# Splitting the first matmul groups by rows of x as they land, and a tail with two adding DMAs

## The chip, the cores and the metric

One program runs on all 8 cores of one Trainium2 chip, each core with one sequence of its own. The metric is the device time of the slowest core in microseconds (us). All times here are of fast runs: executions in which one die is slower than the other at a lower clock, as the program sometimes has them, are left out. A core's *span* is the time from its first to its last instruction in the records; the time of an execution was 1.5 to 2.7 us above its longest span.

## The reference, cut to what matters

One layer of a decoder trunk. Each core takes 2080 tokens of 1024 channels:

```python
h = rmsnorm(x, g_pre_mix)
z = h @ w_in                          # 4096 columns: u, v, b, c and two gates
...                                   # pooling mixer and gated short convolution, merged by gates
x = x + rmsnorm(merged @ w_o, g_post_mix)
h = rmsnorm(x, g_pre_ffn)
upc, new_ffn = causal_dwconv(h @ w_up, buf_ffn, w_ffn_conv)     # 2 x 2816 columns
gate, val = jnp.split(upc, 2, axis=-1)
y = (jax.nn.silu(gate) * val) @ w_down
x = x + rmsnorm(y, g_post_ffn)
```

## The kernel before

Channels lie on the partitions. A tile of x is 8 rows (k = 0 to 7) of 128 channels. In the mixer the tokens come in five tiles (512, then 392 each). A group is 8 matmuls, one for each k, into one PSUM bank. The first five groups of tiles 0 and 1 use x scaled but not yet normed (`RAW`), so they don't wait for the sums of squares.

```python
def win_group(t, jj, b, lo, hb):
    N = TA[t]
    wb = W_IN.ap[:, jj, :].rearrange("p (k c) -> p k c", k=KC)
    pe([(bank(b, N, lo), wb[:, k, :], hb.ap[:, k, lo:N]) for k in range(KC)], [W_IN.t(jj, 1), hb.t()],
       [("ps", b)], N - lo)
...
wd = [wload(W_IN, w_in, 0, 1, BL)]
wd += [wload(W_IN, w_in, i, 1, BL, after=[xs0[1]]) for i in range(1, 16)]   # after x's second pair of rows
...
seq = [(0, i) for i in range(NRAW, M0)] + [(1, i) for i in range(NRAW)] + [(0, i) for i in range(M0, M1)]
for t, i in seq:
    F_block(t, i)          # one group each, and its eviction
```

PE's order is fixed, so the first group of tile 1 stands still until all 8 rows of tile 1's x have landed and are converted, and all that follows waits behind it. The first group behind the 40 matmuls of tile 1 is tile 0's ninth; its start is the end of the head.

The weights of the second half (`w_up`, 44 blocks of 256 KB) are loaded block by block while the last mixer tiles run:

```python
def wup(n):
    ...
    pool_dma(dst.flat, w_up[:, i * BL:k * BL], [], [dst.t()], 128 * (k - i) * BL * 4, mx=2048,
             after=[last_pe[0]])
```

The tail of the last tile multiplies 8 rows of y by the norm and adds the residual: two rows by an adding DMA (GpSimd issues it, the DMA adds to what lies in memory), six by adds on DVE and POOL with plain writes behind them:

```python
for q in range(4):
    yq = Y.ap[:, 2 * q:2 * q + 2, :]
    dve(... out=yq, in0=yq, in1=sdb, op=ALU.mult ...)
    if q == 0:
        pool_dma(yT[:, 0:2, lo:lo + NB], yq, ..., acc=True)
        continue
    for k, n, add in ((2 * q, 2, (pool_tt, dve)[q - 1]),) if q < 3 else ((6, 1, dve), (7, 1, pool_tt)):
        add(... out=yk, in0=yk, in1=X1.ap[:, k:k + n, :], op=ALU.add ...)
        sp_dma(yT[:, k:k + n, lo:lo + NB], yk, ...)
```

Of the kernel before, what the change touches and what calls it, by code (L numbers as in the profile page):

```python
# [62 lines left out]
class Sched:  # L63
# [55 lines left out]
    def order(self):  # L119
# [29 lines left out]
        tab = None  # L149
# [130 lines left out]
def build_nc():  # L280
# [257 lines left out]
    def prenorm_sq(t, q):  # L538
        sq = XSQ2[0] if t == 0 else H[t]
        N = TA[t]  # L540
        act(lambda e: e.activation(out=sq.ap[:, 2 * q:2 * q + 2, 0:N], in_=X[t].ap[:, 2 * q:2 * q + 2, :], func=AF.Square),
            [X[t].t(2 * q, 2)], [sq.t(2 * q, 2)], 2 * N)

# [16 lines left out]
    def win_group(t, jj, b, lo, hb):  # L560
        N = TA[t]
        wb = W_IN.ap[:, jj, :].rearrange("p (k c) -> p k c", k=KC)
        pe([(bank(b, N, lo), wb[:, k, :], hb.ap[:, k, lo:N]) for k in range(KC)], [W_IN.t(jj, 1), hb.t()],
           [("ps", b)], N - lo)
# [83 lines left out]
    def F_block(t, i):  # L648
        kind, c = FSEQ[i]
        N = TA[t]  # L650
        lo = lo_of(t, {"u": 0, "b": LO}.get(kind, LOP))
        raw = t < 2 and i < NRAW
        b = next_bank()
        win_group(t, i, b, lo, RAW[t] if raw else H[t])
# [200 lines left out]
    def epi_y(t):  # L855
# [7 lines left out]
        if t == NTB - 1:  # L863
            for q in range(4):
                yq = Y.ap[:, 2 * q:2 * q + 2, :]
                dve(lambda e, yq=yq: e.tensor_tensor(out=yq, in0=yq, in1=sdb, op=ALU.mult),  # L866
                    [Y.t(2 * q, 2), ("ps", SB)], [Y.t(2 * q, 2)], 2 * NB, psum=True, pri=-40000.0 + 4000 * q)
                if q == 0:
                    pool_dma(yT[:, 0:2, lo:lo + NB], yq, [Y.t(0, 2)], [("yo", t, q)], 2 * 128 * 2 * NB * 4, acc=True)
                    continue  # L870
                for k, n, add in ((2 * q, 2, (pool_tt, dve)[q - 1]),) if q < 3 else ((6, 1, dve), (7, 1, pool_tt)):
                    yk = Y.ap[:, k:k + n, :]
                    add(lambda e, yk=yk, k=k, n=n: e.tensor_tensor(out=yk, in0=yk, in1=X1.ap[:, k:k + n, :], op=ALU.add),  # L873
                        [Y.t(k, n), X1.t(k, n)], [Y.t(k, n)], n * NB)
                    sp_dma(yT[:, k:k + n, lo:lo + NB], yk, [Y.t(k, n)], [("yo", t, k)], 128 * n * NB * 4)
# [24 lines left out]
    def warm(n):  # L900
# [4 lines left out]
    xs0 = [sp_dma(X[0].flat[:, 0:2 * N0], xT[0][:, 0:2 * N0], [], [X[0].t(0, 2)], 128 * 2 * N0 * 4,  # L905
                  pri=-1e6)]
    sp_dma(CST, cst, [], [KCST], 128 * 256 * 4, pri=-9e5)
    for q in range(1, 4):
        xs0.append(sp_dma(X[0].flat[:, 2 * q * N0:2 * (q + 1) * N0], xT[0][:, 2 * q * N0:2 * (q + 1) * N0], [],
                          [X[0].t(2 * q, 2)], 128 * 2 * N0 * 4, pri=-8e5 + q))  # L910
# [4 lines left out]
    wd += [wload(W_IN, w_in, i, 1, BL, after=[xs0[1]]) for i in range(1, 16)]  # L915
# [10 lines left out]
    for q in range(4):  # L926
        prenorm_sq(0, q)
        for k in (2 * q, 2 * q + 1):
            dve(lambda e, k=k: e.tensor_scalar(out=RAW[0].ap[:, k, :], in0=X[0].ap[:, k, :], scalar1=cc(C_G1 + k), scalar2=None,
                                               op0=ALU.mult), [X[0].t(k, 1), KCST], [RAW[0].t(k, 1)], N0, rate=2.0)  # L930
    for q in range(4):
        pe([(bank(SB, N0), ONES, XSQ2[0].ap[:, k, :]) for k in (2 * q, 2 * q + 1)], [ONESB.t(), XSQ2[0].t(2 * q, 2)],
           [("ps", SB)], N0, start=q == 0, stop=q == 3)
        if q < 3:
            warm(20)
    ln_exp(0, N0, sq=1)
    for i in range(NRAW):
        F_block(0, i)
# [14 lines left out]
    for i in range(NRAW, 16):  # L953
        seq += [(1, i)] + ([(0, M1 + i - NRAW)] if M1 + i - NRAW < 16 else [])
    for t, i in seq:
        F_block(t, i)
# [225 lines left out]
```

## Time and profile before

| | before |
|---|---|
| time, median of the first runs | 826.05 us (825.92 to 827.45) |
| the profiled execution | 824.09 us, spans 816.9 to 822.5 us |
| start of tile 0's ninth group, by core | 39.1 to 44.9 us, mean 41.6 |
| PE's idle time before tile 1 | 1.5 to 4.4 us, mean 3.0 |
| from that start to the end of the last matmul | 766.6 to 768.7 us, mean 767.1 |
| tail: from there to the last landing | 10.6 to 11.0 us |

The last three rows of times sum to a core's span but for some 0.3 us. They are read from the trace core by core: **head**, **middle**, **tail**. The page itself shows the slowest core alone.

### The profile page before, as it was taken

The page shows a single profiled execution, that of the slowest core. Times are in us where ns is not written, and L with a number is a line of the kernel's source. Part 1 is how long each engine was busy: PE and PEld are TensorE (multiplying, and loading weights), DVE is VectorE, ACT ScalarE, POOL GpSimd, SP SyncE. Part 2 cuts the span into 40 slices and gives each one's busy share as a digit, 9 for nine tenths or more (in the row PEclk, how much of TensorE's full clock was granted, in tenths as well). Part 3 has the DMA queues.
Part 4 walks back from the last instruction along what each step waited for, and adds up shares of the span by engine and source line. Part 5 has one row for each costly group of instructions (what it writes and reads, how often), then busy time and mean ns, then how long its engine had stood idle before and what let it go on. Part 6 is the DMA issues. An engine that isn't in the chain of part 4 may idle for free.

```text
span 822.5 us, 16751 instructions; the slowest of 8 cores (816.9 to 822.5 us)
## 1 busy us (share of the span) xinstructions
PE 799.4 (97%) x5138; PEld 499.5 (61%) x5138; DVE 565.1 (69%) x1054; ACT 452.1 (55%) x902; POOL 262.8 (32%) x297
## 2 busy tenths in 40 slices
PE   6799999999999999999999999999999999999994
PEld 5355445555555555666666666666666666666662
DVE  3788438896895867688996476568566765785723
ACT  3333265666565555676765475456556554665532
POOL 5543001001201243489642243225222522242231
PEclk9899999999999999999999999999999999999998
DMA  8999803845125789999970033015101500050063
GB/s 164 200 159 155 145 25 89 214 130 129 64 75 102 140 135 216 202 161 158 195 128 1 16 56 61 1 36 70 37 2 36 70 2 1 3 68 2 1 136 74
DMA packets 62839, 75.18 MB, mean 91 GB/s; under 512 B 3072, under 2 KB 59264, under 8 KB 62736
## 3 DMA queue, kind: packets, MB, share of 16 engines
q0 software_dynamic: 41440, 44.97, 37.9%
q1 hardware_dynamic: 21312, 29.14, 11.7%
q8 instruction: 44, 0.72, 0.3%
q14 instruction: 43, 0.35, 0.2%
HBM read 81.53 MB, written 22.90 MB: 127 GB/s over the span
## 4 chain that ended last, share of the span: by engine, by line
PE 94%; DMA 3%; POOL 1%; DVE 1%; issue 0%; DVEq 0%; ACT 0%; SPq 0%; ACTq 0%; POOLq 0%
PE ps L469 94%; DMA big<-xT 3%; POOL big L482 1%; DVEq L1053 0%; DVE big L866 0%; DVE big L784 0%; ACT big L849 0%; SPq L476 0%; DVE big L822 0%; ACT big L524 0%; ACT ps L527 0%; DVE big L947 0%; DVE big L873 0%; DVEq L272 0%; ACTq L272 0%
## 5 line engine op out<-in xcount | busy, mean ns | idle before, releaser
L469 PE MATMUL ps<-big 128*128 128x346 bf16 (+6 forms) x5138 | 799.4, 319 | 12.1 <-DVE big L947 4.4
L469 PEld LDWEIGHTS ps<-big 128*128 128x128 bf16 x5138 | 499.5, 98 | 311.8 <-issue 18.4
L822 DVE SCALAR_TENSOR_TENSOR big<-ps,big 128x344 f32<-128x344 f32 (+1 forms) x528 | 281.4, 569 | 95.3 <-ACT big L818 74.6
L836 POOL TENSOR_TENSOR big<-big 128x344 bf16<-128x344 f32 x132 | 125.3, 950 | 257.1 <-DVE big L822 181.2
L818 ACT ACTIVATE big<-ps,big 128x344 f32<-128x344 f32 (+1 forms) x264 | 139.4, 541 | 66.6 <-PE ps L469 60.9
L835 ACT ACTIVATE big<-big 128x344 f32<-128x344 f32 x132 | 64.6, 490 | 47.5 <-DVE big L822 45.5
L701 ACT ACTIVATE big<-ps 128x392 f32<-128x392 f32 (+1 forms) x80 | 39.3, 514 | 54.0 <-PE ps L469 34.8
L480 POOL DMA_DIRECT2D big<-xT x16 | 15.7, 1005 | 158.0 <-DVE big L714 151.0
L846 ACT ACTIVATE big<-ps,big 128x344 f32<-128x344 f32 x48 | 26.0, 546 | 57.1 <-PE ps L469 54.9
L482 POOL DMA_DIRECT2D big<-w_up x44 | 33.5, 768 | 58.1 <-PE ps L469 48.6
L714 DVE SCALAR_TENSOR_TENSOR big<-ps,big 128x392 f32<-128x392 f32 (+1 forms) x40 | 25.8, 645 | 35.2 <-PE ps L469 32.1
L513 DVE TENSOR_TENSOR big<-big 128x1568 bf16<-128x1568 bf16 (+3 forms) x28 | 24.4, 873 | 29.1 <-ACT big L733 28.5
L480 POOL DMA_DIRECT2D yT<-big x21 | 27.4, 1540 | 31.6 <-DVE big L866 17.1
L852 DVE TENSOR_TENSOR big<-big 128x688 bf16<-128x688 bf16 x17 | 8.8, 517 | 40.6 <-ACT big L849 40.6
L731 ACT ACTIVATE big<-ps,big 128x392 f32<-128x392 f32 (+1 forms) x40 | 24.5, 612 | 14.2 <-PE ps L469 13.6
L610 DVE TENSOR_TENSOR big<-big 128x406 f32<-128x406 f32 (+7 forms) x50 | 29.8, 597 | 1.6 <-DVE big L616 0.2
L482 POOL DMA_DIRECT2D big<-w_in x32 | 23.1, 741 | 23.7 <-DMA big<-w_in 12.2
L579 ACT ACTIVATE big<-big 128x392 f32<-128x392 f32 (+1 forms) x20 | 12.8, 638 | 30.2 <-DVE big L665 30.1
L553 DVE SCALAR_TENSOR_TENSOR big<-big 128x392 bf16<-128x392 f32 (+1 forms) x40 | 24.2, 645 | 6.1 <-ACT big L595 3.2
L849 ACT ACTIVATE big<-ps 128x344 bf16<-128x344 f32 x48 | 21.6, 450 | 11.3 <-PE ps L469 11.3
L582 DVE SCALAR_TENSOR_TENSOR big<-big 128x392 f32<-128x392 f32 (+1 forms) x40 | 25.3, 642 | 3.3 <-ACT big L579 2.3
L720 DVE TENSOR_TENSOR big<-big 128x392 bf16<-128x392 f32 (+1 forms) x40 | 24.9, 632 | 2.3
(60 smaller groups left out, 351.0 us busy)
## 6 DMA issues: line engine op xcount, KB each, us to landing
big<-w_up POOLq DMA_DIRECT2D x44, 256.0 KB, 9.9
big<-w_in POOLq DMA_DIRECT2D x32, 256.0 KB, 23.1
yT<-big POOLq DMA_DIRECT2D x21, 344.0 KB, 6.3
big<-xT POOLq DMA_DIRECT2D x16, 392.0 KB, 7.6
yT<-big SPq DMA_DIRECT2D x8, 784.0 KB, 8.0
big<-w_dn POOLq DMA_DIRECT2D x8, 704.0 KB, 14.6
big<-xT SPq DMA_DIRECT2D x6, 784.0 KB, 5.6
big<-h2T SPq DMA_DIRECT2D x6, 692.0 KB, 4.9
```

What stands on the lines that cost most here:

```text
L469: ins = e.matmul(o, lhsT=l, rhs=x, start=(start and i == 0), stop=(stop and i == last))
L480: return S.add("pool", lambda e: e.dma_start(out=out, in_=in_, accum_op=ALU.add, max_dma_last_dim=mx), r, w, dma=True, byts=byts, pri=pri, ...
L482: return S.add("pool", lambda e: e.dma_start(out=out, in_=in_, max_dma_last_dim=mx), r, w, dma=True, byts=byts, pri=pri, after=after)
L582: dve(lambda e, k=k: e.scalar_tensor_tensor(out=cv, in0=p[:, 2 + k + lo:2 + k + N], scalar=cc(C_WC + 4 * k + c), in1=cv, op0=ALU.mult, op1 ...
L610: dve(lambda e, nx=nx, cur=cur, s=s, a2=a2: e.tensor_tensor(out=nx[:, a2:W], in0=cur[:, a2:W], in1=cur[:, a2 - s:W - s], op=ALU.add), [ct] ...
L701: act(lambda e, b=b, g=g: e.activation(out=GT[t].ap[:, g, lo:N], in_=bank(b, N, lo), func=AF.Sigmoid), [("ps", b)], [GT[t].t(g, 1)], N, ps ...
L714: dve(lambda e: e.scalar_tensor_tensor(out=A_, in0=bank(bp, N, lo), scalar=cc(C_PS + m), in1=A_, op0=ALU.mult, op1=ALU.mult), [("ps", bp), ...
L818: act(lambda e, b=b, fj=fj, tt=tt: e.activation(out=tt[:, 0:n], in_=bank(b, n), func=AF.Copy, scale=cc(C_WF + fj)), [("ps", b), KCST], [to ...
L822: dve(lambda e, b=b, fj=fj, tt=tt, k=k: e.scalar_tensor_tensor(out=tt[:, 0:n], in0=ps[:, b * 512 + k:b * 512 + k + n], scalar=cc(C_WF + 44 ...
L835: act(lambda e: e.activation(out=g, in_=g, func=AF.Silu), [T.t(0, 1)], [T.t(0, 1)], NB, tab="silu")
L836: S.add("pool", lambda e: e.tensor_tensor(out=gb.ap[:, j, :], in0=g, in1=v, op=ALU.mult), [T.t()], [gb.t(j, 1)], dur=NB * 2.17 + 100)
L846: act(lambda e: e.activation(out=Y.ap[:, m, :], in_=bank(b, NB), func=AF.Copy, scale=cc(C_G4 + m)), [("ps", b), KCST], [Y.t(m, 1)], NB, ps ...
```

## The change

Its intent: (1) run tile 1's first four groups by rows as they land, in four banks; (2) release two blocks of w_in earlier; (3) cut the last pair of tile 0's rows in two; (4) in the tail, let multiplies and adds go through PSUM, so DVE and POOL don't stop one another, and give two more rows to a second adding DMA.

```diff
-    pe([(bank(b, N, lo), wb[:, k, :], hb.ap[:, k, lo:N]) for k in range(KC)], [W_IN.t(jj, 1), hb.t()],
-       [("ps", b)], N - lo)
+    pe([(bank(b, N, lo), wb[:, k, :], hb.ap[:, k, lo:N]) for k in range(k0, k1)], [W_IN.t(jj, 1), hb.t(k0, k1 - k0)],
+       [("ps", b)], N - lo, start=k0 == 0, stop=k1 == KC)
...
+PARTS0 = ((0, 2), (2, 2), (4, 2), (6, 1), (7, 1))          # rows of tile 0's x, one DMA each
-wd += [wload(W_IN, w_in, i, 1, BL, after=[xs0[1]]) for i in range(1, 16)]
+wd += [wload(W_IN, w_in, i, 1, BL, after=[xs0[0 if i < 3 else 1]]) for i in range(1, 16)]
...
+    if k == 6:
+        win_group(0, 0, b0, F_lo(0, 0), RAW[0], 0, 6)
...
 for t, i in seq:
-    F_block(t, i)
+    if (t, i) == (1, 0):
+        bs = {(1, c): next_bank() for c in range(4)}
+        for k0, k1 in ((0, 4), (4, 6), (6, 8)):
+            for (_, c), b in bs.items():
+                win_group(1, c, b, F_lo(1, c), RAW[1], k0, k1)
+    F_block(t, i, bs.get((t, i)))
...
+steps = ((0, 2, None, "acc"), (2, 2, None, "acc"), (7, 1, None, "pool"), (4, 2, 0, "dve"), (6, 1, 2, "dve"))
...      # "acc": adding DMA; "pool": POOL adds in SBUF; "dve": multiply into bank 0 or 2, add from it
```

More of the change, by code (lines that the diff above doesn't have):

```diff
@@ L148, in order @@
         ends = {"sp": [0.0] * 14, "pool": [0.0] * 16}
-        tab = None
+        tab = "ln"
         cold = 0.0
@@ L538, in prenorm_sq @@
     def prenorm_sq(t, q):
-        sq = XSQ2[0] if t == 0 else H[t]
+        sq = H[t]
         N = TA[t]
@@ L558, in lo_of, with win_group @@
         return lo if t == 0 else 0
-    def win_group(t, jj, b, lo, hb):
+    def win_group(t, jj, b, lo, hb, k0=0, k1=KC):
         N = TA[t]
         wb = W_IN.ap[:, jj, :].rearrange("p (k c) -> p k c", k=KC)
-        pe([(bank(b, N, lo), wb[:, k, :], hb.ap[:, k, lo:N]) for k in range(KC)], [W_IN.t(jj, 1), hb.t()],
-           [("ps", b)], N - lo)
+        pe([(bank(b, N, lo), wb[:, k, :], hb.ap[:, k, lo:N]) for k in range(k0, k1)], [W_IN.t(jj, 1), hb.t(k0, k1 - k0)],
+           [("ps", b)], N - lo, start=k0 == 0, stop=k1 == KC)
     cv_rr = [0] * NTA
@@ L646, in load_states, with F_lo, F_block @@
                     [ST_POOL.t(c, 1)], [RED.t(c, 1)], NS * w)
-    def F_block(t, i):
+    def F_lo(t, i):
+        return lo_of(t, {"u": 0, "b": LO}.get(FSEQ[i][0], LOP))
+    def F_block(t, i, b=None):
         kind, c = FSEQ[i]
-        N = TA[t]
-        lo = lo_of(t, {"u": 0, "b": LO}.get(kind, LOP))
+        N, lo = TA[t], F_lo(t, i)
         raw = t < 2 and i < NRAW
-        b = next_bank()
-        win_group(t, i, b, lo, RAW[t] if raw else H[t])
+        if b is None:
+            b = next_bank()
+            win_group(t, i, b, lo, RAW[t] if raw else H[t])
         src = bank(b, N, lo)
@@ L863, in epi_y @@
         if t == NTB - 1:
-            for q in range(4):
-                yq = Y.ap[:, 2 * q:2 * q + 2, :]
-                dve(lambda e, yq=yq: e.tensor_tensor(out=yq, in0=yq, in1=sdb, op=ALU.mult),
-                    [Y.t(2 * q, 2), ("ps", SB)], [Y.t(2 * q, 2)], 2 * NB, psum=True, pri=-40000.0 + 4000 * q)
-                if q == 0:
-                    pool_dma(yT[:, 0:2, lo:lo + NB], yq, [Y.t(0, 2)], [("yo", t, q)], 2 * 128 * 2 * NB * 4, acc=True)
-                    continue
-                for k, n, add in ((2 * q, 2, (pool_tt, dve)[q - 1]),) if q < 3 else ((6, 1, dve), (7, 1, pool_tt)):
-                    yk = Y.ap[:, k:k + n, :]
-                    add(lambda e, yk=yk, k=k, n=n: e.tensor_tensor(out=yk, in0=yk, in1=X1.ap[:, k:k + n, :], op=ALU.add),
-                        [Y.t(k, n), X1.t(k, n)], [Y.t(k, n)], n * NB)
-                    sp_dma(yT[:, k:k + n, lo:lo + NB], yk, [Y.t(k, n)], [("yo", t, k)], 128 * n * NB * 4)
+            steps = ((0, 2, None, "acc"), (2, 2, None, "acc"), (7, 1, None, "pool"), (4, 2, 0, "dve"), (6, 1, 2, "dve"))
@@ new lines, in epi_y @@
+            for i, (k, n, b, _) in enumerate(steps):
+                yk = Y.ap[:, k:k + n, :]
+                out = yk if b is None else ps[:, b * 512:(b + n) * 512].rearrange("p (c n) -> p c n", c=n)[:, :, 0:NB]
+                dve(lambda e, yk=yk, out=out, n=n: e.tensor_tensor(
+                    out=out, in0=yk, in1=bank(SB, NB).unsqueeze(1).to_broadcast([128, n, NB]), op=ALU.mult),
+                    [Y.t(k, n), ("ps", SB)], [Y.t(k, n)] if b is None else [("ps", b + r) for r in range(n)], n * NB,
+                    pri=-80000.0 + 8000 * i)
@@ new lines, in epi_y @@
+            for k, n, b, how in steps:
+                yk, xk = Y.ap[:, k:k + n, :], X1.ap[:, k:k + n, :]
+                if how == "acc":
+                    pool_dma(yT[:, k:k + n, lo:lo + NB], yk, [Y.t(k, n)] + [("y", a, 0) for a in tiles_a(lo, lo + NB)],
+                             [("yo", t, k)], 2 * 128 * n * NB * 4, acc=True)
+                    continue
+                if how == "pool":
+                    pool_tt(lambda e, yk=yk, xk=xk: e.tensor_tensor(out=yk, in0=yk, in1=xk, op=ALU.add),
+                            [Y.t(k, n), X1.t(k, n)], [Y.t(k, n)], n * NB)
+                else:
+                    src = ps[:, b * 512:(b + n) * 512].rearrange("p (c n) -> p c n", c=n)[:, :, 0:NB]
+                    dve(lambda e, yk=yk, xk=xk, src=src: e.tensor_tensor(out=yk, in0=src, in1=xk, op=ALU.add),
+                        [("ps", b + r) for r in range(n)] + [X1.t(k, n)], [Y.t(k, n)], n * NB)
+                sp_dma(yT[:, k:k + n, lo:lo + NB], yk, [Y.t(k, n)], [("yo", t, k)], 128 * n * NB * 4)
@@ L904, in build_nc @@
     N0 = TA[0]
-    xs0 = [sp_dma(X[0].flat[:, 0:2 * N0], xT[0][:, 0:2 * N0], [], [X[0].t(0, 2)], 128 * 2 * N0 * 4,
-                  pri=-1e6)]
-    sp_dma(CST, cst, [], [KCST], 128 * 256 * 4, pri=-9e5)
-    for q in range(1, 4):
-        xs0.append(sp_dma(X[0].flat[:, 2 * q * N0:2 * (q + 1) * N0], xT[0][:, 2 * q * N0:2 * (q + 1) * N0], [],
-                          [X[0].t(2 * q, 2)], 128 * 2 * N0 * 4, pri=-8e5 + q))
+    PARTS0 = ((0, 2), (2, 2), (4, 2), (6, 1), (7, 1))
+    xs0 = []
+    for q, (k, m) in enumerate(PARTS0):
+        xs0.append(sp_dma(X[0].flat[:, k * N0:(k + m) * N0], xT[0][:, k * N0:(k + m) * N0], [], [X[0].t(k, m)],
+                          128 * m * N0 * 4, pri=-2e6 + 4e4 * q))
+        if q == 0:
+            sp_dma(CST, cst, [], [KCST], 128 * 256 * 4, pri=-2e6 + 2e4)
     S.add("pool", lambda e: e.memset(ONES, 1.0 / D), [], [ONESB.t()], dur=200)
@@ L925, in build_nc @@
     warm(60)
-    for q in range(4):
-        prenorm_sq(0, q)
-        for k in (2 * q, 2 * q + 1):
-            dve(lambda e, k=k: e.tensor_scalar(out=RAW[0].ap[:, k, :], in0=X[0].ap[:, k, :], scalar1=cc(C_G1 + k), scalar2=None,
-                                               op0=ALU.mult), [X[0].t(k, 1), KCST], [RAW[0].t(k, 1)], N0, rate=2.0)
-    for q in range(4):
-        pe([(bank(SB, N0), ONES, XSQ2[0].ap[:, k, :]) for k in (2 * q, 2 * q + 1)], [ONESB.t(), XSQ2[0].t(2 * q, 2)],
-           [("ps", SB)], N0, start=q == 0, stop=q == 3)
-        if q < 3:
+    b0 = next_bank()
+    for k, m in PARTS0:
+        act(lambda e, k=k, m=m: e.activation(out=XSQ2[0].ap[:, k:k + m, :], in_=X[0].ap[:, k:k + m, :], func=AF.Square),
+            [X[0].t(k, m)], [XSQ2[0].t(k, m)], m * N0)
+        for r in range(k, k + m):
+            dve(lambda e, k=r: e.tensor_scalar(out=RAW[0].ap[:, k, :], in0=X[0].ap[:, k, :], scalar1=cc(C_G1 + k), scalar2=None,
+                                               op0=ALU.mult), [X[0].t(r, 1), KCST], [RAW[0].t(r, 1)], N0, rate=2.0)
+    for k, m in PARTS0:
+        if k == 6:
+            win_group(0, 0, b0, F_lo(0, 0), RAW[0], 0, 6)
+        pe([(bank(SB, N0), ONES, XSQ2[0].ap[:, r, :]) for r in range(k, k + m)], [ONESB.t(), XSQ2[0].t(k, m)],
+           [("ps", SB)], N0, start=k == 0, stop=k == 7)
+        if k < 4:
             warm(20)
     ln_exp(0, N0, sq=1)
+    win_group(0, 0, b0, F_lo(0, 0), RAW[0], 6, 8)
     for i in range(NRAW):
-        F_block(0, i)
+        F_block(0, i, b0 if i == 0 else None)
         if i == 1:
@@ L954, in build_nc @@
         seq += [(1, i)] + ([(0, M1 + i - NRAW)] if M1 + i - NRAW < 16 else [])
+    bs = {}
     for t, i in seq:
-        F_block(t, i)
+        if (t, i) == (1, 0):
[4 more added lines that the diff above has]
+        F_block(t, i, bs.get((t, i)))
     L = NTA - 1
@@ L1040, in build_nc @@
     lo = T0B + (NTB - 1) * NB
-    sp_dma(X1.ap[:, 2:8, :], yT[:, 2:8, lo:lo + NB], [("y", a, q) for a in tiles_a(lo, lo + NB) for q in range(2)],
-           [X1.t(2, 6)], 128 * 6 * NB * 4)
+    sp_dma(X1.ap[:, 4:8, :], yT[:, 4:8, lo:lo + NB], [("y", a, q) for a in tiles_a(lo, lo + NB) for q in range(1, 2)],
+           [X1.t(4, 4)], 128 * 4 * NB * 4)
     for m in range(8):
```

## The prediction

> **What bounds the kernel now.** I read the spans of all cores first, then the page's busy shares and chain, then the matmul engine's timeline of the first 50 us, the evictions' and conversions' timelines beside it, and the last 15 us. The metric is the slowest core, and the cores differ:
>
> ```profile
> core 0: 818.5 us, clock 0.993
> core 1: 822.5 us, clock 0.991
> ...
> core 4: 816.9 us, clock 0.995
> ...
> core 6: 822.0 us, clock 0.991
> ```
>
> Cores 1 and 6 set the time. The page shows core 1:
>
> ```profile
> PE 799.4 (97%) x5138; PEld 499.5 (61%) x5138; DVE 565.1 (69%) x1054; ACT 452.1 (55%) x902; POOL 262.8 (32%) x297
> ...
> PE ps L469 94%; DMA big<-xT 3%; POOL big L482 1%; DVEq L1053 0%; DVE big L866 0%; DVE big L784 0%; ACT big L849 0%; SPq L476 0%; DVE big L822 0%; ACT big L524 0%; ACT ps L527 0%; DVE big L947 0%; DVE big L873 0%; DVEq L272 0%; ACTq L272 0%
> ```
>
> PE is busy 97%, so only the two ends are left to win, and the change adds or removes no matmul except a warm-up batch. At the head, PE's timeline of core 1:
>
> ```profile
> 14.08 3.83 PE L469 MATMUL ps<-big 128*128 128x512 bf16 x32 [0.48 <-ACT big L541]
> 18.29 1.85 PE L469 MATMUL ps<-big 128*128 128x500 bf16 x8 [0.38 <-DMA big<-w_in]
> 20.85 10.42 PE L469 MATMUL ps<-big 128*128 128x500 bf16 x48 [0.71 <-DMA big<-w_in]
> 35.63 14.74 PE L469 MATMUL ps<-big 128*128 128x392 bf16 x67 [4.36 <-DVE big L947]
> ```
>
> The eight groups of tile 0 end at 31.27; then PE idles 4.36 us until L947 has converted the last row of tile 1's x. The windows show what that idle time does afterwards (columns: stretch, length, busy time of PE, PEld, DVE, ACT, POOL, then granted clock, DMA share, GB/s):
>
> ```profile
> 31.00:33.00 2.00, 0.27 (x2) 0.00 (x0) 1.55 (x4) 1.82 (x3) 1.11 (x2) 1.00 1.04 217
> 33.00:35.00 2.00, 0.00 (x0) 0.00 (x0) 1.44 (x4) 1.99 (x4) 0.59 (x2) 0.65 1.14 173
> 35.00:37.00 2.00, 1.37 (x5) 0.69 (x6) 1.97 (x4) 2.00 (x6) 1.38 (x2) 0.50 1.17 163
> 37.00:39.00 2.00, 2.00 (x8) 0.92 (x7) 2.00 (x4) 0.87 (x3) 0.56 (x1) 0.50 1.20 179
> 39.00:41.00 2.00, 2.00 (x10) 0.92 (x8) 1.62 (x3) 0.00 (x0) 0.70 (x1) 0.64 1.10 150
> ```
>
> The clock falls to half and stays there until about 40.2: the first 14 matmuls start 327 ns apart, the later ones 166 ns. So the wait costs 4.36 us and then about 14 x 0.16 = 2.3 us more. DMA share is above 1 throughout: x of tile 1 is late because the transfers are full, and no reordering on PE makes it land earlier.
>
> The tail of core 1:
>
> ```profile
> 811.21 0.31 PE L469 MATMUL ps<-big 128*128 128x344 bf16 x1 [0.32 <-ACT big L849]
> 811.61 0.55 ACT L524 ACTIVATE big<-ps,big 128x344 f32<-128x344 f32 x1
> 812.25 0.46 ACT L527 ACTIVATE ps<-big 128x344 f32<-128x344 f32 x1
> ...
> 814.24 1.22 POOL L480 DMA_DIRECT2D yT<-big  x1 [17.14 <-DVE big L866]
> 814.99 2.13 POOL L873 TENSOR_TENSOR big<-big 128x688 f32<-128x688 f32 x1
> 815.94 2.78 DVE L873 TENSOR_TENSOR big<-big 128x688 f32<-128x688 f32 x1
> ```
>
> The last matmul ends at 811.5. The DVE add of 688 columns takes 2.78 us, where the multiplies of the same size take 0.86: it stands still while POOL's add runs. The last plain DMA is issued at 819.78 and lands at 822.16; the adding DMA issued at 814.24 lands at 819.32.
>
> **What the Trainium skill says.** "TensorE: Matmul & The Clock Gate", Part 1: the array drops to half clock after an idle window of about 3.4 us and needs about as long a busy one to come back. The trace agrees: 4.36 us idle, then 0.50 for some 4.6 us of matmuls; the idle time of 0.71 us at 20.85 costs no clock. "SBUF — State Buffer", Who interferes with whom: a DVE instruction with two SBUF inputs and a GpSimd one that reads SBUF exclude each other for a whole instruction, and with one SBUF input there is no conflict. The trace agrees: 2.78 us for the add, 0.86 us for the multiply with a PSUM input that runs beside the same POOL add. "DMA: Bandwidth & Descriptors", SWDGE vs HWDGE vs iDMA: accumulating goes through GpSimd's software queue only, so both adding DMAs share one queue. The trace agrees in that all adding DMAs are on q0.
>
> **The change, part by part.**
>
> 1. Tile 1 split. Its first four groups run as k 0 to 3 for all four, then 4 and 5, then 6 and 7, in four banks. The x pairs of core 1 land at 30.14, 31.69, 33.05 and 34.44 by the trace, and ACT's conversion (0.62 us, L944) ends last: 32.40 for k 3, 33.8 for k 5, 35.4 with DVE for k 7. 16 matmuls at 0.166 from 32.55 end at 35.2; 8 more end at 36.5, 8 more at 37.85; the fifth group (8) ends at 39.2; two sums make 39.5. Before, tile 0's ninth group starts at 44.94. Gain 5.4 us. The idle time left is some 1.3 us, too short by the above to lose the clock. The same sum for core 6 (x at 29.6, 30.5, 31.8, 33.4; 44.13 before) gives 38.3, a gain of 5.8. Core 3 idles only 1.5 us here and cannot gain as much: its 40 matmuls after 31.9 end at 38.9 with the sums, against 40.38, and part 3 may add 1. It goes from 819.9 to about 817.4, and core 1 to 817.1. So the slowest core gains about 5.1.
>
> 2. Two blocks of w_in released by x's first quarter. Block 1 is issued at 11.18 because x's second pair lands at 10.61; now it can go at about 7.7. Blocks 1 and 2 land at 18.16 and 20.71, and PE waits 0.38 and 0.71 us for them. But x and block 0 fill the DMA then (share near 1), and block 0, first in the same software queue, lands only at 13.24. So the pair moves by perhaps 1 to 2 us on core 1, where the share drops to 0.42 in 12 to 14 us, and by little on core 0, where it stays above 1. It fills at most 1.2 us of idle DMA. Credit: 0.3 us for the slowest core, since PE then only waits longer for tile 1.
>
> 3. Tile 0's last pair cut in single rows, six of eight matmuls of its first group ahead of them. The Square behind the last row shrinks from 1.06 to about 0.6 us, and six matmuls (1.3 us) move ahead. PE gains 1 to 1.5 us here, but blocks 3 to 7 arrive just in time already (0.13 to 0.6 us of slack), and tile 1's x comes after them. Worth nothing alone on core 1, about 1 us on core 3.
>
> 4. DVE behind the gain. Before, PE reaches the bank of tile 1's first group 2.8 us after it is free, that of the third 2.0 us after. Now PE is 5.4 us earlier, while DVE can start only when tile 1's sums are through: at 40.9 or so instead of 43.86, 2.9 us earlier. 2.0 + 2.9 - 5.4 = -0.5: a wait of about 0.5 us. From 54 us on the slack is 4.6 us or more, and w_in from block 8 lands 9 us ahead, so the rest survives. Head in all: 5.1 + 0.3 - 0.5 = 4.9 us.
>
> 5. Tail. The multiplies into PSUM and the adds from it have one SBUF input, so the stall of some 1.9 us ends: three full multiplies (0.79 apart), two half ones (0.43), one full and one half add, from 812.81, end near 817.3 instead of 819.1. The last plain DMA then lands near 820.5. But the second adding DMA takes its place: with two issued back to back elsewhere (561.14 and 561.90, landing at 567.09 and 568.87; 638.98 and 639.77, landing at 643.82 and 646.24) the second lands 1.8 to 2.4 us behind the first and 7.3 to 7.7 us after the first's issue. From 814.24 that is 821.5 to 821.9, plus something for the plain writes among them, against 822.16. Gain 0.4 us.
>
> **The rivals.** (a) The tail's second adding DMA ends later than today's last DMA: the four issued from 792.20 on had their second land 8.7 us after the first issue, which would be 822.9, a loss of 0.8. (b) DVE or ACT becomes the bound in 40 to 60 us: DVE is busy nearly all of 44 to 61, and if the static order puts tile 1's sums late, two or three of the five microseconds go. For it: in this kernel the sums ran 4 us after their input was ready. Against it: 3.2 us of DVE idle just before, and the growing slack. Time about 824. (c) The early w_in blocks slow tile 0's rows of x, PE idles longer at 10 to 15 us and starts half-clocked, as core 3 does (0.50 at 16 to 18 us): 1 to 2 us lost there, 822.5. (d) The split only moves idle time, because x is hidden anyway; it would be 825. The halved clock and the 5 us of slack behind it speak against this.
>
> **Range and chances.** 4.9 + 0.4 = 5.3 us from 826.1 gives 820.8. Downward, the spans of all cores drop by up to 7 if the DMA shift counts: 818.5. Upward, rivals (a) and (b) together: 823.6. Two per cent is 16.5 us, more than all idle time at both ends that the change touches, so "within 2%" is near certain.
>
> **What would show it.** PE's idle time before the first 392-column matmuls falls from 4.36 to below 2 us on core 1 and the clock stays 1.00 in 33 to 41 us (step 1); tile 0's ninth group starts near 39 to 40. A new PE wait of about half a microsecond on DVE near 46 us (step 4). DVE's adds in the tail take under 0.9 us, and the last landing is that of an adding DMA, 10 us or more behind the last matmul (step 5; 10.65 before). The cores should lie closer together than 816.9 to 822.5. Wrong would be: a half clock still there, a new wait of over 2 us after 40 us, or a tail shorter than 9.5 us.

## The result, and the profile after

The changed kernel took **824.64 us** (median of 4 runs, 823.69 to 825.42) against 826.05. The ratio is 0.9979, with a 95% interval of 0.9961 to 0.9996. Ratios here are the mean time of one kernel's fast runs over that of the other's fast runs of the same rounds, so not quite the ratio of the medians. The kernel is 1.4 us faster, 1.8 us in the means, not 5.3, and its time lies above the stated range.

Spans of the changed kernel's cores:

```profile
core 0: 821.8 us, clock 0.992
...
core 5: 823.0 us, clock 0.993
core 6: 816.0 us, clock 0.995
```

Another core is the slowest, and the spans lie no closer together than before (7.0 us now, 5.6 before). The page's busy times, and its chain by line:

```profile
PE 798.9 (97%) x5118; PEld 499.1 (61%) x5118; DVE 562.9 (68%) x1055; ACT 450.1 (55%) x903; POOL 262.5 (32%) x297
...
PE ps L469 87%; DMA big<-xT 3%; POOL big L839 1%; POOL big L482 1%; POOL big L687 0%; ACT big L821 0%; POOL big L767 0%; DVE big L825 0%; DVE big L553 0%; ACT L524 0%; POOLq L1078 0%; ACT big L524 0%; SPq L476 0%; POOL big L764 0%; ACT big L772 0%
```

PE's work is the same but for 20 warm-up matmuls. In the chain its share fell from 94% to 87%: evictions and loads of the middle (POOL L839, L687 and L482, ACT L821, DVE L825) stand in it now. The head of core 5 on PE:

```profile
11.81 1.71 PE L469 MATMUL ps<-big 128*128 128x512 bf16 x22 [1.14 <-ACT big L942]
14.57 2.07 PE L469 MATMUL ps<-big 128*128 128x512 bf16 x9 [1.06 <-ACT big L942]
18.62 28.12 PE L469 MATMUL ps<-big 128*128 128x512 bf16 x133 [1.98 <-ACT big L942]
47.28 4.96 PE L469 MATMUL ps<-big 128*128 128x392 bf16 x26 [0.54 <-DVE big L662]
```

From 18.62 on PE runs 133 matmuls without a gap, right through the place where it stood before tile 1. At 47.28 stands the short new wait for DVE, 0.54 us; it falls into the middle. The three waits for L942 (the Square of tile 0's rows) show that PE still stands for tile 0's x. The windows of the same core (stretch, length, busy times of PE, PEld, DVE, ACT and POOL, granted clock, DMA share, GB/s):

```profile
18.00:20.00 2.00, 1.38 (x4) 0.57 (x5) 0.64 (x1) 1.29 (x3) 2.00 (x4) 0.72 1.11 150
...
33.00:35.00 2.00, 2.00 (x14) 1.18 (x13) 2.00 (x4) 1.86 (x5) 0.76 (x2) 1.00 1.17 170
```

The clock is full at 33 to 35, but on this core a shorter stretch of half clock (0.72 in these 2 us) now lies behind the wait for tile 0's last row. That wait is only 1.98 us long. In the first trace of before a wait of 2.21 us on core 3 cost the clock as well (0.65 in 14 to 16 us), while one of 2.86 us on core 2 didn't (1.00 in 32 to 34 us): the limit of about 3.4 us, which the prediction took over, doesn't tell these waits apart. The tail of core 5:

```profile
809.61 0.31 PE L469 MATMUL ps<-big 128*128 128x344 bf16 x1 [0.32 <-ACT big L852]
...
812.70 2.45 POOL L480 DMA_DIRECT2D yT<-big  x2 [17.26 <-DVE big L871]
...
814.24 1.85 POOL L882 TENSOR_TENSOR big<-big 128x344 f32<-128x344 f32 x1
814.41 1.29 DVE L886 TENSOR_TENSOR big<-ps,big 128x688 f32<-128x688 f32 x2
816.17 2.19 SPq L476 DMA_DIRECT2D yT<-big  x3
```

DVE's two adds now take 1.29 us together: the stall is gone as predicted, and DVE ends at 815.7, 5.8 us behind the last matmul. But the three plain writes, issued at 816.17 to 817.14, land only at 821.02, 822.18 and 822.63, some 5 to 5.5 us later, where before they took 2.4 to 3.1 us. The last landing is a plain write, 12.7 us behind the last matmul (10.65 before). Queues and issues in 808 to 823 us, the kernel before, then the changed one (packets, MB, share of 16 engines; then KB and median us to landing):

```profile
q1 hardware_dynamic: 832, 1.06, 19.4%
q0 software_dynamic: 272, 0.35, 19.2%
```

```profile
q0 software_dynamic: 544, 0.70, 36.2%
q1 hardware_dynamic: 560, 0.70, 12.9%
...
yT<-big POOLq DMA_DIRECT2D x2, 344.0 KB, 6.5
yT<-big SPq DMA_DIRECT2D x2, 172.0 KB, 5.2
yT<-big SPq DMA_DIRECT2D x1, 344.0 KB, 5.5
```

One adding DMA moves 0.35 MB in 19.2% of 15 us of all engines, that is 2.9 us of all 16; the plain writes moved 1.06 MB in the same share, so 0.97 us for each 0.35 MB. The second adding DMA is thus three times the transfer work of what it replaces, and the plain writes stand in line beside it.

Head, middle and tail of the two traces, in us (mean of 8 cores, and the slowest core):

| | before, mean | after, mean | before, core 1 | after, core 5 |
|---|---|---|---|---|
| head | 41.55 | 38.13 | 44.94 | 39.75 |
| middle | 767.07 | 769.08 | 766.57 | 770.16 |
| tail | 10.78 | 12.48 | 10.65 | 12.72 |

So the head gained 5.2 us on the slowest cores, as foreseen. The middle, whose work the change doesn't touch, gave 3.6 back (0.5 of it is the new wait at 47 us) and the tail 2.1. PE's and POOL's instructions come in the same order in the middle of both kernels, those of ACT and DVE from about 83 us on. The experiments ask what these two losses are.

### The profile page after: what moved, and what is told of

Read it like the earlier page. It is cut to its first block, busy times and chain, and to the rows that moved or that the text cites. A ratio compares the mean times of both kernels' runs of the same rounds, so it can differ in the third digit from the quotient of the medians.

```text
span 823.0 us, 16725 instructions; the slowest of 8 cores (816.0 to 823.0 us)
## 1 busy us (share of the span) xinstructions
PE 798.9 (97%) x5118; PEld 499.1 (61%) x5118; DVE 562.9 (68%) x1055; ACT 450.1 (55%) x903; POOL 262.5 (32%) x297
## 4 chain that ended last, share of the span: by engine, by line
PE 87%; DMA 3%; POOL 2%; issue 2%; ACT 2%; DVE 1%; POOLq 0%; SPq 0%; ACTq 0%; DVEq 0%
PE ps L469 87%; DMA big<-xT 3%; POOL big L839 1%; POOL big L482 1%; POOL big L687 0%; ACT big L821 0%; POOL big L767 0%; DVE big L825 0%; DVE big L553 0%; ACT L524 0%; POOLq L1078 0%; ACT big L524 0%; SPq L476 0%; POOL big L764 0%; ACT big L772 0%
## 5 line engine op out<-in xcount | busy, mean ns | idle before, releaser
L469 PE MATMUL ps<-big 128*128 128x346 bf16 (+5 forms) x5118 | 798.9, 319 | 11.1 <-ACT big L942 4.2
L825 DVE SCALAR_TENSOR_TENSOR big<-ps,big 128x344 f32<-128x344 f32 (+1 forms) x528 | 281.6, 569 | 94.0 <-ACT big L821 73.5
L839 POOL TENSOR_TENSOR big<-big 128x344 bf16<-128x344 f32 x132 | 125.4, 951 | 260.3 <-DVE big L825 184.8
L821 ACT ACTIVATE big<-ps,big 128x344 f32<-128x344 f32 (+1 forms) x264 | 138.8, 542 | 63.6 <-PE ps L469 57.2
L480 POOL DMA_DIRECT2D big<-xT x16 | 15.7, 1008 | 154.7 <-DVE big L717 147.8
L482 POOL DMA_DIRECT2D big<-w_up x44 | 33.4, 764 | 57.3 <-PE ps L469 50.5
L482 POOL DMA_DIRECT2D big<-w_in x32 | 23.3, 745 | 21.6 <-DMA big<-w_in 11.9
L579 ACT ACTIVATE big<-big 128x392 f32<-128x392 f32 (+1 forms) x20 | 12.7, 638 | 31.9 <-DVE big L668 31.7
L852 ACT ACTIVATE big<-ps 128x344 bf16<-128x344 f32 x48 | 21.6, 451 | 12.7 <-PE ps L469 12.7
L553 DVE SCALAR_TENSOR_TENSOR big<-big 128x392 bf16<-128x392 f32 (+1 forms) x40 | 24.3, 646 | 3.7 <-ACT big L530 2.0
L787 DVE SCALAR_TENSOR_TENSOR big<-big 128x392 bf16<-128x392 f32 (+1 forms) x40 | 24.9, 657 | 2.7 <-ACT big L527 2.7
## 6 DMA issues: line engine op xcount, KB each, us to landing
big<-w_up POOLq DMA_DIRECT2D x44, 256.0 KB, 10.8
```

What stands on the lines that cost most here:

```text
L469: ins = e.matmul(o, lhsT=l, rhs=x, start=(start and i == 0), stop=(stop and i == last))
L480: return S.add("pool", lambda e: e.dma_start(out=out, in_=in_, accum_op=ALU.add, max_dma_last_dim=mx), r, w, dma=True, byts=byts, pri=pri, ...
L482: return S.add("pool", lambda e: e.dma_start(out=out, in_=in_, max_dma_last_dim=mx), r, w, dma=True, byts=byts, pri=pri, after=after)
L821: act(lambda e, b=b, fj=fj, tt=tt: e.activation(out=tt[:, 0:n], in_=bank(b, n), func=AF.Copy, scale=cc(C_WF + fj)), [("ps", b), KCST], [to ...
L825: dve(lambda e, b=b, fj=fj, tt=tt, k=k: e.scalar_tensor_tensor(out=tt[:, 0:n], in0=ps[:, b * 512 + k:b * 512 + k + n], scalar=cc(C_WF + 44 ...
L839: S.add("pool", lambda e: e.tensor_tensor(out=gb.ap[:, j, :], in0=g, in1=v, op=ALU.mult), [T.t()], [gb.t(j, 1)], dur=NB * 2.17 + 100)
```

## The experiments

The kernel before ran too. "Mean span" is the mean over all cores and all fast timed runs, a far steadier number than the time; for the kernel before it was 821.91, 821.96, 821.88 and 821.63, for the changed kernel 820.03 and 820.52.

**Parts alone.** `old_tail`: the changed kernel with the tail of before.

```diff
-steps = ((0, 2, None, "acc"), (2, 2, None, "acc"), (7, 1, None, "pool"), (4, 2, 0, "dve"), (6, 1, 2, "dve"))
...
+for q in range(4):          # the tail of before, and its loads of X1 rows 2 to 7
```

> The changed kernel with the tail of the kernel before (one adding DMA, adds in SBUF, load of X1 rows 2 to 7). Theory (the new tail costs: its two adding DMAs fill the DMA engines, so plain writes land 5 us after issue instead of 2.5): the stretch from the last matmul to the last landing falls from 12.6 back to about 10.7 us on every core, and the time falls by 1.9 to about 822.7. Rival (the tail is neutral and the lost gain went elsewhere, in the middle): 824.6, unchanged.

It took 823.46 us (median of the fast runs, as for all that follow), ratio 0.9961 (0.9944 to 0.9978), mean span 818.71, tail 10.6 to 11.2 us.

`tail_only`: the kernel before with the new tail.

```diff
+steps = ((0, 2, None, "acc"), (2, 2, None, "acc"), (7, 1, None, "pool"), (4, 2, 0, "dve"), (6, 1, 2, "dve"))
-for q in range(4):          # the head stays that of before
```

> The kernel before with the new tail alone. Theory (the new tail costs about 1.9 us by itself): 828.0, last matmul to last landing 12.5 us, the head untouched (PE idle 3 to 4 us before tile 1). Rival (tail neutral or a gain of 0.4 as predicted): 825.7 to 826.1.

It took 828.81 us, ratio 1.0020 (1.0007 to 1.0033): slower than before by 1.9 us in the means. Mean span 823.33, tail 12.1 to 13.3 us. So **the new tail is a loss**. By these two runs it costs 0.9 to 1.9 us of the time (each kernel against the kernel before), by the traces 1.7.

`split_only`: the kernel before with tile 1's split alone.

```diff
+        for k0, k1 in ((0, 4), (4, 6), (6, 8)):
+            for (_, c), b in bs.items():
+                win_group(1, c, b, F_lo(1, c), RAW[1], k0, k1)
```

> The kernel before with the split of tile 1's first four groups alone. Theory (the split is what gains at the head, some 4 us on the slowest core): PE's idle time before tile 1 below 1.5 us, no half clock in 33 to 41 us, tile 0's ninth group at 37 to 39.5 instead of 39.5 to 44.9. If the middle passes all of it on, 821 to 822; if the DMA-bound stage of the w_up loads (280 to 345 us) eats part of it, as the landings of the changed kernel suggest, 822.5 to 824. Rival (the other parts of the head made the gain): 825 or more.

It took 823.47 us, ratio 0.9958 (0.9941 to 0.9976), 3.3 us in the means; mean span 818.83. The head ended at 37.0 to 40.7 us, mean 38.9. The split gives all that the head gives: `old_tail` with every other part of the head added is no better. In three of its cores PE waited 0.6 to 3.8 us near 110 us for x of the next tile: on core 0 its last part was issued at 98.80 and landed at 108.78, just before the Square and the adds that PE then waited for. `split_one` has such waits on four cores, the changed kernel has none, so the other parts of the head may save something here that they lose elsewhere. The program's fixed order also differs from that of before on PE at 162 to 164 us, so the split isn't quite the only difference.

`late_w12`: the changed kernel, with blocks 1 and 2 of w_in released as before.

```diff
-    wd += [wload(W_IN, w_in, i, 1, BL, after=[xs0[0 if i < 3 else 1]]) for i in range(1, 16)]
+    wd += [wload(W_IN, w_in, i, 1, BL, after=[xs0[1]]) for i in range(1, 16)]
```

> The changed kernel with w_in blocks 1 and 2 released by x's second part again. Theory (the early blocks take DMA time from x's rows of tile 0): the last row of tile 0 lands 1.5 to 2.5 us earlier than in the changed kernel (15.4 to 17.9 there), PE starts tile 0 earlier, but tile 1's rows land when they did, so tile 0's ninth group starts at most 1 us earlier and the time falls by 0 to 1 us (823.6 to 824.6). Rival (the early release pays, as intended): blocks 1 and 2 land later, PE waits for them, 0.5 to 1.5 us slower.

Ratio 0.9990 (0.9976 to 1.0003), mean span 820.58, that is the changed kernel's. Tile 0's last row landed at 14.6 us in the mean, against 16.7 in the changed kernel and 14.0 before: the early blocks do hold up x by 2 us. But the head ended at 38.4 us, with them at 38.1. What x loses the weights gain; the two runs' intervals overlap, and no gain or loss is shown.

`cut_only`: the kernel before with the row cut of tile 0 alone (the six matmuls ahead and the 20 warm-up matmuls less belong to it).

```diff
+    PARTS0 = ((0, 2), (2, 2), (4, 2), (6, 1), (7, 1))
-    wd += ... after=[xs0[0 if i < 3 else 1]]
-        if (t, i) == (1, 0):          # no split of tile 1
```

> The row cut of tile 0 alone: no split of tile 1, no early blocks of w_in, the tail of before. Theory (the cut gives nothing, since PE then only waits longer for tile 1's x): ninth group of tile 0 at 41 to 42.5 us in the mean of the cores (41.7 in before), mean span of the timed runs 821.5 to 822.3 us (821.9 for before), ratio 0.999 to 1.001; and the part of the time that no span covers (time less longest span: 1.5 to 1.7 us in before, up to 2.6 us in the kernels with the new head) shows values over 2 us here as well. Rival: the cut gains its 1 us of PE start: ratio 0.9985 or below, and the uncovered part stays at 1.5 to 1.7.

It took 826.36 us, ratio 1.0005 (0.9980 to 1.0030), mean span 821.85, head 41.7 us. The cut alone is worth nothing, and the PE timeline of its slowest core shows why:

```profile
34.47 17.73 PE L469 MATMUL ps<-big 128*128 128x392 bf16 x86 [3.85 <-ACT big L953]
```

PE starts tile 0 earlier and waits 3.85 us for tile 1. The other half of what I expected was wrong: the time less the longest span stayed at 1.5 to 1.6 us in all its fast runs. It stays at 1.5 to 1.7 in the kernel before, in `tail_only` and in the three kernels with the split alone as well; only kernels with the row cut and the split together show values up to 2.7 (2.0 in the mean of all, 2.2 and 2.35 in the changed kernel). This costs the changed kernel 0.6 to 0.8 us outside all spans. Its cause stays open.

**The tail.** `one_add`: the changed kernel with one adding DMA; rows 2 to 6 go through PSUM and DVE.

```diff
-steps = ((0, 2, None, "acc"), (2, 2, None, "acc"), (7, 1, None, "pool"), (4, 2, 0, "dve"), (6, 1, 2, "dve"))
+steps = ((0, 2, None, "acc"), (7, 1, None, "pool"), (2, 2, 0, "dve"), (4, 2, 2, "dve"), (6, 1, 4, "dve"))
```

> The changed kernel with one adding DMA in the tail (rows 0 and 1), rows 2 to 6 multiplied into PSUM and added by DVE from there, row 7 on POOL. Theory (it is the second adding DMA that costs): DVE ends its adds near 6.7 us after the last matmul, the plain writes land 2.5 to 3 us after issue, last matmul to last landing about 9.7 us, 2.9 below the changed kernel and 1 below the kernel before; time some 2.9 us below the changed kernel. Rival (the writes are late for another reason, say the PSUM adds or the order of issue): 12 us and no gain.

It took 823.93 us, ratio 0.9951 (0.9934 to 0.9969). The tail was 10.8 to 11.1 us: the loss is gone, but it isn't the 9.7 us I had hoped for. Counted from the eviction of the last matmul (L524), its last write is issued 1.7 us earlier than that of `old_tail` (6.58 against 8.24 us) and lands at the same moment (10.85 in both, mean of the cores): its writes take 3.2 to 4.7 us each, where those of `old_tail` take 2.3 to 4.0 (means 4.1 and 2.8). What DVE gains is lost in flight.

`after_again`: the changed kernel without an edit, for the same rounds.

> The changed kernel once more, on the same chip as the others of this call, as their reference. Expected: 0.998 of the kernel before, last matmul to last landing 12.6 us, and in the trace the pairs of neighbouring cores (0 and 1, 2 and 3, 4 and 5, 6 and 7) whose matmuls run within 1 us of each other show PE waits of 2 us or more between 250 and 420 us, the pairs more than 2.5 us apart under 1 us.

825.29 us, ratio 0.9972 (0.9953 to 0.9991): the first result stands. All fast runs of `one_add` (822.9 to 824.2) are below all of these (825.0 to 825.6). What I expected of the pairs could hardly be seen in this trace: no pair ran within 1 us, and the one 3 us apart had waits of 1.14 and 0.24 us, not both under 1.

`k7_last`: row 7's write is issued behind the other two.

```diff
-            for k, n, b, how in steps:
+            for k, n, b, how in steps[:2] + steps[3:] + steps[2:3]:
...
-                sp_dma(yT[:, k:k + n, lo:lo + NB], yk, [Y.t(k, n)], [("yo", t, k)], 128 * n * NB * 4)
+                sp_dma(yT[:, k:k + n, lo:lo + NB], yk, [Y.t(k, n)] + ([("ps", 2)] if k == 7 else []), [("yo", t, k)], 128 * n * NB * 4)
```

> The changed kernel with the plain write of row 7 issued last instead of first, so that the other two no longer stand behind POOL's add. Theory (contention with the second adding DMA sets the landing): the first write is issued 0.8 us earlier but the last landing moves by less than 0.5 us. Rival (the wait in the issue order sets it): the tail falls by 0.8 us, to 11.8.

825.23 us, ratio 0.9974 (0.9956 to 0.9992), tail 11.7 to 13.7 us. Counted from the issue of the first adding DMA, the three writes go out 0.8 us earlier than in the changed kernel (2.66 to 3.64 us against 3.47 to 4.44), and the last of them lands no earlier (9.8 against 9.7, mean of the cores), after some 6 us of flight each. The time of issue isn't what holds them.

`no_add`: no adding DMA at all; rows 0 to 6 through PSUM and DVE, row 7 on POOL.

```diff
+steps = ((7, 1, None, "pool"), (0, 2, 0, "dve"), (2, 2, 2, "dve"), (4, 2, 4, "dve"), (6, 1, 6, "dve"))
```

> Changed kernel with no adding DMA in its tail: rows 0 to 6 through PSUM and DVE, row 7 on POOL, all written plainly. Theory (an adding DMA is the costly part of the tail): DVE's last add ends 0.8 to 0.9 us later than with one adding DMA, but the writes land some 2.5 us after their issue, so the tail from last matmul to last landing is 9.7 to 10.3 us (10.8 to 11.1 with one adding DMA, 11.9 to 13.0 with two), ratio 0.994. Rival: DVE's longer chain and the plain writes among themselves set the end: tail 11 us or more, ratio 0.995 to 0.996.

823.43 us, ratio 0.9962 (0.9942 to 0.9982), tail 10.2 to 10.8 us, mean 10.6. The queue in 808 to 823 us:

```profile
q1 hardware_dynamic: 1104, 1.41, 26.3%
```

The same 1.41 MB now take 26.3% of the engines' time, against 38.6% before and 49.1% in the changed kernel, and the writes land 1.8 to 3.5 us after their issue. DVE's last add ended 0.8 us later behind the last matmul than with one adding DMA, as expected, and that eats most of the gain. Two, one and no adding DMAs give tails of 12.5, 10.8 to 10.95 and 10.4 to 10.6 us: the step that hurts is the second one.

`one_add_2`, the same file as `one_add`, in the rounds of `no_add` and `split_one`.

> The changed kernel with one adding DMA once more, to have it in the same rounds as the other two: theory 0.9951 as before (0.994 to 0.996), tail 10.7 to 11.1 us. Rival (the first result was luck of a few rounds, and the version is no better than the changed kernel): 0.997 to 0.998.

823.55 us, ratio 0.9963 (0.9948 to 0.9978).

`split_one`: the kernel before with tile 1's split and the tail with one adding DMA (the two edits above, no other).

> Kernel before with the split of tile 1 and the tail with one adding DMA, without the other parts of the head. Theory (those parts give nothing): same as the changed head with that tail, 0.9951, that is 0.994 to 0.996, ninth group of tile 0 at 37 to 40.7 us, tail 10.6 to 11.1 us. Rival (the row cut and the early blocks are worth about 1 us): 0.996 to 0.997.

823.07 us, ratio 0.9963 (0.9947 to 0.9980), mean span 818.24. The row cut and the early blocks aren't needed: no run shows a gain from them.

`split_no`: the split and the tail without adding DMAs.

```diff
+steps = ((7, 1, None, "pool"), (0, 2, 0, "dve"), (2, 2, 2, "dve"), (4, 2, 4, "dve"), (6, 1, 6, "dve"))
```

> Kernel before with the split of tile 1 and a tail without any adding DMA. Theory: best of both, tail 10.4 to 10.8 us, mean span 817.8 to 818.4 us, ratio 0.9950 to 0.9962. Rival (rows 0 and 1, now loaded back with the others at the end, come late or hold up other transfers): tail 11 us or more, ratio 0.997.

824.46 us, ratio 0.9975 (0.9949 to 1.0000). The tail was 10.2 to 10.6 us and the mean span 818.56, about as hoped, but the longest span was on average no shorter (822.7, against 821.7 for `split_one`). It isn't shown to be better than the rest.

**The middle.** The rise from 767.1 to 769.1 us had two readings: the change brings about waits in the middle, or the one trace of before had merely escaped them. `half_wup`: `old_tail` with every second block of w_up loaded 64 columns wide, its neighbour used instead. The result is wrong, the instructions and their order are the same.

```diff
+            m = 64 if i % 2 else BL
-            pool_dma(dst.flat, w_up[:, i * BL:k * BL], [], [dst.t()], 128 * (k - i) * BL * 4, mx=2048,
+            pool_dma(dst.flat[:, 0:m], w_up[:, i * BL:i * BL + m], [], [dst.t()], 128 * (k - i) * BL * 4, mx=2048,
...
-        wb = W_UP.ap(blk).rearrange("p (k c) -> p k c", k=KC)
+        wb = W_UP.ap(blk - blk % 2).rearrange("p (k c) -> p k c", k=KC)
```

> The changed kernel with the old tail, and every second w_up block loaded only in its first 64 columns and replaced by its neighbour in the matmuls (wrong result on purpose, same instructions in the same order, 22 of 44 loads nearly empty). Theory (the PE waits between 250 and 420 us come from DMA that is full in the stage of the w_up loads, worst where the two cores of a pair run in step): those waits fall to under 0.5 us on every core, the write of tile 3's second half lands within 12 us instead of 19 to 23, and the stretch from tile 0's ninth group to the last matmul is 766.5 to 767.5 us on all cores instead of up to 770.7; time 1.5 to 3 us below the same kernel with full loads (0.996 of the kernel before there), so 0.993. Rival (the waits are the instruction order's own): they stay.

820.34 us, ratio 0.9918 (0.9897 to 0.9939). The middle fell to 767.6 us in the mean, PE's waits from 250 to 420 us to 0.3 us on every core, and the spans came together (the write of the fourth tile's second half landed after 11.8 to 15.7 us, where I had put 12):

```profile
core 0: 817.0 us, clock 0.992
...
core 5: 817.7 us, clock 0.992
```

So the waits of the middle, and with the new head most of the differences among the cores, are those of a stage in which the transfers of w_up fill the DMA.

`before_half`: the same edit of the loads in the kernel before.

> Kernel before with every second block of w_up loaded at an eighth of its width (the neighbour's weights are used, wrong on purpose). Theory: in the kernel before, the waits of the middle appear only on the one pair of cores that runs in step (2.06 and 1.50 us on cores 2 and 3; 0.43 to 0.51 us elsewhere) and the slowest core is not of it, so half the transfers give it little: ratio 0.998 to 1.000, waits from 250 to 420 us of 0.3 to 0.5 us on all cores. Rival: fewer transfers help any version alike, by the 3.6 us that they were worth on top of the new head (0.9918 against 0.9961): ratio 0.9957.

824.14 us, ratio 0.9974 (0.9957 to 0.9990). The value fits neither expectation: 2.4 us gained where I had put 0 to 1.7, and where the rival had 3.6; its interval, 0.8 to 3.6 us, excludes neither clearly. The kernel before pays for this stage too, though its cores still differ without it (816.6 to 821.9 us), since their heads do. In the mean span the halved loads are worth 1.5 us on the kernel before and 1.0 us on the new head, in the time 2.4 and 3.5 us, each against the kernel before. What the change adds to the middle by this measure is between nothing and 1.1 us, and the intervals of these runs are wider than that.

`before_p2` and `before_p3`: the kernel before without an edit, for two more traces.

> The kernel before, unchanged, for a second trace. Theory (the profiled execution of before was a lucky one: 824.1 us against 825.9 to 827.5 of the timed ones, and from the start of tile 0's ninth group to the last matmul its cores took 767.0 us in the mean): this one shows the waits of the middle too: 768.5 to 769.5 us in the mean of the cores, two pairs or more with waits of over 1 us per core from 250 to 420 us, spans of 821 to 823 us in the mean. Rival (before is free of these waits, and the changed kernel's earlier matmuls bring them about): 766.6 to 767.5 us, spans near 820.

> The same once more, since one execution is one draw: the two theories as for the second trace. If this and the second trace fall on different sides, the middle's waits are a matter of the draw, and only the timed runs' spans decide.

They took 828.41 and 827.90 us, their cores 768.6 and 768.1 us in the middle (mean), where the first trace has 767.1. The first of them fits the theory at its lower edge, the other falls between the two. Spans of `before_p2`:

```profile
core 1: 816.2 us, clock 0.996
...
core 4: 826.9 us, clock 0.990
```

Its slowest core, on PE (from 333 us on) and by its waits from 320 to 340 us (engine, line, what for: us in total, times, longest):

```profile
333.45 68.57 PE L469 MATMUL ps<-big 128*128 128x392 bf16 x455 [0.52 <-ACT big L701]
402.89 13.54 PE L469 MATMUL ps<-big 128*128 128x346 bf16 x90 [0.87 <-DVE big L822]
417.68 7.63 PE L469 MATMUL ps<-big 128*128 128x346 bf16 x51 [1.25 <-DVE big L822]
```

```profile
ACT big L769 <- DMA big<-xT: 3.3, 2, 1.9
```

PE waits for ACT and DVE at the same three places of the program as in the changed kernel (there at 328.6, 397.1 and 411.9 us, for 0.53, 0.21 and 1.38 us), and ACT has waited 3.3 us for x of the fourth tile. This x comes by an adding DMA, which GpSimd issues among the w_up loads at 311.67 and which lands at 323.96. In the profile's chain (300 to 335 us: start, length, what) PE's stop at 333.45 goes back to it:

```profile
311.67 12.30 DMA big<-xT
...
324.05 0.87 ACT big L769
```

The same DMA takes 12.3 us here, 12.0 on the slowest core of the changed kernel, 9.8 on that of the first trace, and 8.2 to 8.3 on those with half the loads. The trace that the prediction rested on was a lucky one: its slowest core went through the middle without a stop, and its time of 824.09 us lay below all the timed runs beside it. Over all five traces without the split the middle took 768.0 us in the mean, so the changed kernel's 769.1 is 1.1 us more, and 0.6 of that is the new wait near 47 us. The rest, some 0.5 us, is what the stage of the w_up loads can have taken.

Which cores wait can be read from the pairs 0 and 1, 2 and 3, 4 and 5, 6 and 7. For 16 traces of kernels with the full w_up (64 pairs), this is PE's waiting time from 250 to 420 us, both cores summed, by how far apart in time the two cores of the pair run (the same matmul near 250 us, each core counted from its own first instruction):

| distance | pairs | waits, mean us | least, most |
|---|---|---|---|
| under 1 us | 21 | 5.6 | 3.6, 8.0 |
| 1 to 2 us | 14 | 3.5 | 1.0, 6.4 |
| 2 to 3 us | 13 | 2.4 | 0.4, 5.0 |
| over 3 us | 16 | 0.9 | 0.4, 1.9 |

The correlation is -0.83; cores put together otherwise (0 with 4, 0 with 2, 1 with 2 and so on) give -0.2 to -0.4. It rests on both cores of a pair starting at once, which the records don't show: their own time stamps lie 12 us to 15 ms apart. The Trainium skill's "HBM Reference", Specifications (TRN2), says that the two cores of a pair share a memory stack, which would make them each other's rivals when they ask for the same blocks at the same time; no run here shows where they meet. Without the split the pairs are 2.45 us apart in the mean and wait 2.7 us, with it 1.7 us apart and 3.6 us: some 0.5 us more for each core. It may be that the split makes the cores alike, and by that brings them into step. This is a correlation: the program is the same on all cores, and I found no way to shift one core of a pair alone.

## Why the prediction was wrong

**Tail: the term that failed outright.** "The last plain DMA then lands near 820.5. But the second adding DMA takes its place", gain 0.4 us. The DVE part was right. Wrong was the flight time of the plain writes: I kept the 2.4 us that they had beside one adding DMA, and they took 4.9 to 5.5 beside two. With `tail_only`, `old_tail` and the traces the term is a loss of 0.9 to 1.9 us. It is rival (a) with another last one: it gave the loss as 0.8 us and named the adding DMA, while the last landing was a plain write. I had counted what lands when, queue by queue, and not the engine time that an adding DMA takes from all others, 2.9 us of all 16, though the share stood in the trace of before.

**Head: the mechanism right, the sum too large.** Step 1 held where it was worked out: no half clock at 33 to 41 us, 0 to 1 us of idle time left before tile 1, the ninth group at 39.75 us on the slowest core, 5.2 us earlier. Step 4's wait of "about 0.5 us" came as 0.54 (it is there in all traces with the early blocks and in none without them, 0.03 us; why, no run shows). Steps 2 and 3 are worth nothing measurable (0.3 predicted); rival (c) was right in that x of tile 0 lands 2 us later, and wrong in that it costs. But the head of 4.9 us came out as 3.3 (`split_only`) and 3.0 (`old_tail`). Two things were wrong in it.

The first is "So the slowest core gains about 5.1". It takes the core with the latest head of one execution and lets the rest be equal. In four traces with the old head it ended at 42.0 us in the mean, and the mean core gains 3.9, not 5. And the slowest core is made by head and middle together: in the timed runs of `split_only` the longest span fell by 3.3 us and the mean span by 3.1.

The second is "From 54 us on the slack is 4.6 us or more ... so the rest survives". I had checked the slack to 60 us and not the stage from 275 to 420, where PE hardly waited in that one trace although the DMA share was above 1. Cores that come earlier and more in step wait there: the pairs give 0.5 us for each core, the five traces without the split as much, the halved loads nothing to 1.1. That the waits come from this stage is shown; that the new head adds to them is only made likely.

**The sum.** Some -3.2 us of head and some +1.4 us of tail make -1.8, the measured difference of the means (each figure is about the middle of its two measures, so the sum is no test of its own). Of the 3.5 us that are missing from 5.3, the tail is 1.8 and the head 1.7. The sign that I had named for a wrong tail, one shorter than 9.5 us, pointed the wrong way.

The best kernels are those with the split and one adding DMA or none: `one_add` (0.9951 and 0.9963), `split_one` (0.9963) and `no_add` (0.9962). They beat the kernel before, and `one_add` beat the changed one in the same rounds. Among themselves they are not told apart.

## What to carry to other kernels

A gain read from the slowest core of one trace is a gain on that draw: take several traces, work with the mean over the cores, and ask which stage makes the slowest core next. A stage with a full DMA and no waits in one trace may have no slack in the next. Before giving a row to another DMA, count the engine time that it takes from the transfers beside it, not only its own landing.

## What the Trainium skill lacked or had wrong

- "DMA: Bandwidth & Descriptors", SWDGE vs HWDGE vs iDMA, says who can issue an accumulating DMA, not what it costs: here 0.35 MB took 2.7 to 3.0 us of all 16 engines, against some 1.0 us for the same bytes written plainly. It has no size either for what it does to its neighbours: plain writes of 172 to 344 KB landed 1.8 to 3.5 us after their issue with no adding DMA, 3.1 to 4.7 us when the first of them was issued 2.2 us behind one, and 4.2 to 7.3 us with two.
- "HBM Reference" says that the two cores of a pair share the bandwidth of their memory, not what that costs a core whose DMA is full: here PE's waits from 250 to 420 us, both cores summed, were 5.6 us where the cores run under 1 us apart and 0.9 us over 3. Whether the memory is where they meet, no run shows. The GB/s of the windows (138 to 231 on the slowest cores of the two first traces, 300 to 420 us) can't be set against the page's bandwidth: the weights are read as f32 and written as bf16, and the profile counts a block of w_up as 256 KB, the size as written.
